# First mixer of a two-layer trunk: a group's outputs are issued in pieces between the next group's weight blocks, and VectorE's steps of the solve get precedence

## The chip, the cores and the metric

The kernel runs on one core of one Trainium2 chip. The metric is the device time of one execution in microseconds (us). Engines in the text: TensorE (PE in the rows, with PEld for its weight loads), VectorE (DVE), ScalarE (ACT), GpSimd (POOL) and SyncE (SP), which here only issues transfers.

## The reference

The program is a decoder trunk of two layers on 256 tokens of width 2048, in float32. The change is in the mixer of the first layer, a gated delta rule:

```python
qkv, z, a, b = jnp.split(x @ w_in, ...)
qkv = jax.nn.silu(causal_dwconv(qkv, conv_w))
q, k = l2norm(q) * GDN_DK ** -0.5, l2norm(k)
...
lmat = jnp.where(strict, einsum(kb, k) * decay, 0.0)
sol  = triangular_solve(lmat + eye, rhs, lower=True, unit_diagonal=True)
...
v_new = u_n - einsum(w_n, S)
o_n   = einsum(qd_n, S) + einsum(qk_n, v_new)
...
o = o * rsqrt(mean(square(o)) + RMS_EPS) * norm_g * silu(z)
return o @ w_o
```

There are 32 value heads and 16 key heads of 128; then follow layer norm, a gated feed-forward part, a second mixer (sparse attention) and a second feed-forward part, none of which the diff touches.

## The kernel before

All products with weights are done in two parts. A weight block of 512 KB arrives as `raw` (SyncE issues it, line 103), ScalarE rounds it to `hi` (line 107), VectorE makes `lo = raw - hi` (line 108), and TensorE multiplies both. `raw`, `hi` and `lo` have three buffers each, and the two conversions are issued with a large precedence, so they run about three blocks ahead of TensorE. Products with the weights on the left write `mm_ps` (lines 126 and 130), those with the weights on the right write `b_ps` (lines 150, 151 and 154).

The mixer works through eight groups of four value heads. `keys(g)` makes q and k, `front(g)` makes the decays, the triangular blocks and their inverses of 32 x 32 (GpSimd's long chain at lines 505 and 507), `values(g)` makes v from eight weight blocks and transposes it (`v_ps`, `vt`), `zgate(g)` makes the gate z from eight more, `inverses(g)` fetches the small inverses (`pm<-tt`) and multiplies them (`w_ps`), `solve(g)` solves for `u` in two halves a = 0 and 1 (`s_ps`, `y`, `u`), and `outputs(g)` makes for each half the product `o_ps`, its squares (`sqs`, ScalarE), a reciprocal root in small VectorE steps (`rs`, `rt`, lines 243 to 249), the scaled tile `ot`, its transposes `ot_ps`, and the two parts of `oT`, which the projection with `w_o` reads after the mixer.

A scheduler orders the instructions of each engine: among those it thinks ready, the one written first goes first, or the one with precedence. Each engine then works through its list strictly in that order. What the scheduler thinks ready can be late on the chip.

Two details matter below. The tile `qd` has two buffers: the read of the decays of group g + 2 (`qd<-grow`, line 414, on SyncE's list) must wait until `o_ps` of group g has been made, because that reads the old `qd`; and ScalarE's `qo<-qd,go` (line 419) waits for that read. The blocks of `L` go through DRAM to another layout: four stores `lt<-L` (line 489), one load `ld<-lt` (line 492), both on SyncE's list among the weight blocks; then GpSimd starts its chain.

Of the kernel before, what the change touches and what calls it, by code (L numbers as in the profile page):

```python
# [12 lines left out]
ALU = mybir.AluOpType  # L13
# [43 lines left out]
def bcast(ap, n, axis):  # L57

    dims = [list(x) for x in ap.ap]
    dims.insert(axis, [0, n])  # L60
    return bass.AP(tensor=ap.tensor, offset=ap.offset, ap=dims)


class Trunk:
# [313 lines left out]
    def gdn_groups(self, pool, gk, cw, ng, oT, load, gates):  # L378
# [1 line left out]

        nc, t = self.nc, self.t
        w_in = t["gdn_w_in"]
        pm = pool.tile([P, 8, P], F32, tag="pm", name="pm")
        nc.gpsimd.memset(pm, 0.0)
# [5 lines left out]
        h4 = range(4)  # L392
        five = lambda ap: ap.rearrange("p (j r) t -> p j r t", r=2)

        def conv(n0, out):

            def done(n, ps):
                pd = pads[n % 2]
                self.fold(pool, pd[:, 3:], ps)
                ac = pool.tile([P, S], F32, tag="ac", name="ac", bufs=2)  # L400
                w = cw[:, :, n0 + n]
                nc.scalar.activation(ac, pd[:, 3:], AF.Identity, scale=w[:, 3:4])
                for k in (2, 1, 0):
                    nc.vector.scalar_tensor_tensor(ac, pd[:, k:k + S], w[:, k:k + 1], ac, op0=ALU.mult, op1=ALU.add)
                o = out(n)
                nc.scalar.activation(o, ac, AF.Tanh, scale=0.5)
                nc.vector.scalar_tensor_tensor(o, o, 1.0, ac, op0=ALU.add, op1=ALU.mult)
            return done

        def decays(s):  # L410

            g = s["g"]
            dm = s["qd"] = pool.tile([P, 2, 4, P], F32, tag="qd", name="qd", bufs=2)
            nc.sync.dma_start(out=dm, in_=bass.AP(tensor=self.grow.tensor, offset=self.grow.offset + 4 * g * P,
                                                    ap=[[0, P], [32 * P, 2], [1, 4 * P]]))
            do = s["qo"] = pool.tile([P, 4, P], F32, tag="qo", name="qo", bufs=2)
            L = s["L"] = pool.tile([P, 2, 4, P], F32, tag="L", name="L")
            for h in h4:
                nc.scalar.activation(do[:, h], dm[:, 1, h], AF.Exp, bias=self.gout[:, 4 * g + h:4 * g + h + 1])
            for a in range(2):  # L420
                for h in h4:
                    gc = self.gc[:, a, 4 * g + h:4 * g + h + 1]
                    nc.vector.tensor_scalar(L[:, a, h], dm[:, a, h], gc, 0.0, op0=ALU.subtract, op1=ALU.max)
                    nc.vector.tensor_scalar(dm[:, a, h], dm[:, a, h], gc, 0.0, op0=ALU.subtract, op1=ALU.min)
                nc.scalar.activation(L[:, a], L[:, a], AF.Exp, scale=-1.0)
                nc.scalar.activation(dm[:, a], dm[:, a], AF.Exp)
                nc.gpsimd.tensor_tensor(dm[:, a], dm[:, a], bcast(self.tri, 4, 1), op=ALU.mult)

        def keys(g):
            s = {"g": g}  # L430
            q = s["q"] = pool.tile([P, 2, S], F32, tag="q", name="q")
            k = s["k"] = pool.tile([P, 2, S], F32, tag="k", name="k")
            steps = (self.gemm_t_steps(w_in, 2048 + 256 * g, 256, self.xT, conv(16 + 2 * g, lambda n: k[:, n])),
                     self.gemm_t_steps(w_in, 256 * g, 256, self.xT, conv(2 * g, lambda n: q[:, n])))
            if not g:
                for nb in range(4):
                    load(nb)
                    next(steps[0])
                gates()
            for x in steps:  # L440
                self.go_(x)
            return s
# [71 lines left out]
        def mul(lhs, rhs, ps=None, first=True, last=True):  # L514
            ps = ps if ps is not None else self.sp.tile([P, 4, P], F32, tag="bk", name="s_ps")
            for h in h4:
                nc.tensor.matmul(ps[:, h], lhs[:, h], rhs[:, h], start=first, stop=last)  # L517
            return ps
# [8 lines left out]
                mul(s["L"][:, a], pm[:, 4 * a:4 * a + 4, 32:], ps)  # L527
                nc.scalar.activation(W[:, a, :, 32:], ps, AF.Copy)

        def values(s):  # L530
            g, sv = s["g"], s["sv"]
            v = pool.tile([P, 4, S], F32, tag="v", name="v")
            self.gemm_t(w_in, 4096 + 512 * g, 512, self.xT, conv(32 + 4 * g, lambda n: v[:, n]))
            vt = s["vt"] = pool.tile([P, 2, 4, P], F32, tag="vt", name="vt")
            for a in range(2):
                ps = self.sp.tile([P, 4, P], F32, tag="sp", name="v_ps")
                for h in h4:
                    nc.tensor.transpose(ps[:, h], v[:, h, a * P:(a + 1) * P], self.ident)
                for h in h4:
                    nc.scalar.activation(vt[:, a, h], ps[:, h], AF.Identity, scale=sv[:, a, h // 2, h % 2:h % 2 + 1])  # L540
# [10 lines left out]
        def solve(s):  # L551
            vt = s["vt"]
            u = s["u"] = pool.tile([P, 2, 4, P], F32, tag="u", name="u")
            for a in range(2):
                rhs = vt[:, a]
                if a:
                    ps = mul(s["n21"], u[:, 0])
                    for h in h4:
                        nc.vector.scalar_tensor_tensor(rhs[:, h], ps[:, h], s["nc1"][:, h:h + 1], rhs[:, h],
                                                       op0=ALU.mult, op1=ALU.add)  # L560
                y0 = pool.tile([P, 4, P], F32, tag="y0", name="y0")
                nc.scalar.activation(y0, mul(pm[:, 4 * a:4 * a + 4], rhs), AF.Copy)
                y = y0
                for i in range(3):
                    ps = mul(W[:, a], y)
                    y = u[:, a] if i == 2 else pool.tile([P, 4, P], F32, tag="y", name="y", bufs=2)
                    nc.vector.tensor_tensor(y, y0, ps, op=ALU.subtract)

        def outputs(s):

            g, u = s["g"], s["u"]
            ss = pool.tile([P, 2, 2, 2], F32, tag="oss", name="oss", bufs=2)
            f = pool.tile([P, 2, 2, 2], F32, tag="of", name="of", bufs=2)
            for a in range(2):
                ps = self.sp.tile([P, 4, P], F32, tag="bk", name="o_ps")
                for h in h4:
                    if a:
                        nc.tensor.matmul(ps[:, h], s["qo"][:, h], u[:, 0, h], start=True, stop=False)
                    nc.tensor.matmul(ps[:, h], s["qd"][:, a, h], u[:, a, h], start=not a, stop=True)
                sq = pool.tile([P, P], F32, tag="sqs", name="sqs")  # L580
                for h in h4:
                    nc.scalar.activation(sq, ps[:, h], AF.Square, accum_out=ss[:, a, h // 2, h % 2:h % 2 + 1])
                nc.vector.scalar_tensor_tensor(f[:, a], ss[:, a], 1.0 / 128, bcast(s["wq"][:, :, a], 2, 2),
                                               op0=ALU.mult, op1=ALU.add)
                fa = self.rsqrt(pool, f[:, a].rearrange("p j r -> p (j r)"), 4)
                ot = pool.tile([P, 4, P], F32, tag="y", name="ot", bufs=2)
                for h in h4:
                    nc.vector.scalar_tensor_tensor(ot[:, h], ps[:, h], fa[:, h:h + 1], s["zs"][:, a, h * P:(h + 1) * P],
                                                   op0=ALU.mult, op1=ALU.mult)
                ps = self.sp.tile([P, 4, P], F32, tag="bk", name="ot_ps")  # L590
                for h in h4:
                    nc.tensor.transpose(ps[:, h], ot[:, h], self.ident)
                hi = oT[:, 4 * g:4 * g + 4, 0, a * P:(a + 1) * P]
                lo = oT[:, 4 * g:4 * g + 4, 1, a * P:(a + 1) * P]
                nc.scalar.activation(hi, ps, AF.Identity, scale=ng)
                nc.vector.scalar_tensor_tensor(lo, ps, ng, hi.bitcast(F32), op0=ALU.mult, op1=ALU.subtract)

        def front(s):
            decays(s)
            sums(s)  # L600
            blocks(s)

        n = keys(0)
        front(n)
        for g in range(8):
            s = n
            values(s)
            zgate(s)
            if g < 7:
                n = keys(g + 1)  # L610
            inverses(s)
            if g < 7:
                front(n)
            solve(s)
            outputs(s)


    def project(self, pool, src, h, kt, g, b, prepare, side=1):
# [300 lines left out]
```

## Time and profile before

| what | value |
|---|---|
| median of 3 runs (lowest to highest) | 2909.66 us (2909.45 to 2909.71) |
| the profiled execution, time | 2910.35 us |
| its span, first to last instruction | 2908.3 us |
| TensorE matmul busy | 2823.9 us, 97% |
| VectorE busy | 1873.8 us, 64% |
| ScalarE busy | 1394.7 us, 48% |
| GpSimd busy | 399.7 us, 14% |
| mean granted TensorE clock | 0.992 of full |

Busy times are those of the one profiled execution. The mixer takes the first 800 us of the span. Nearly all of the kernel is bound by TensorE, so a change shows in the time only where TensorE itself waits, or where it is made to wait. The `w_ps` of successive groups stand some 89 us apart.

### The profile page before, as it was taken

How to read it: one execution, taken by the hardware profiler on the slowest of the kernel's cores; microseconds unless marked ns; L12 is line 12 of the kernel's file. 1: busy time of each engine (PE TensorE's matmuls, PEld its weight loads, DVE VectorE, ACT ScalarE, POOL GpSimd, SP SyncE). 2: the span in 40 equal slices, each digit the busy share in tenths (PEclk: the TensorE clock that was granted, in tenths of full speed). 3: DMA queues.
4: the chain of work that ended last, by engine and by line, in shares of the span. 5: the costliest groups of instructions: out<-in, count | busy, mean ns of one | idle time of the engine just before them, and what ended most of it. 6: DMA issues, size and time to landing. Idle time of an engine off the chain costs nothing.

```text
span 2908.3 us, 41890 instructions
## 1 busy us (share of the span) xinstructions
PE 2823.9 (97%) x15790; PEld 2444.7 (84%) x15790; DVE 1873.8 (64%) x3148; ACT 1394.7 (48%) x2147; POOL 399.7 (14%) x720
## 2 busy tenths in 40 slices
PE   8799999999799999999999999999999999999998
PEld 6688888888689888888888878888888888888887
DVE  6578777788455666666545665666576666654465
ACT  4445455554333655555433543455365555543353
POOL 1543354543300000000000000120000000000000
PEclk9899999999899999999999999999999999999999
DMA  7555556555375566666655556554556666655555
GB/s 196 152 135 153 160 157 172 156 149 156 95 227 189 168 194 202 206 205 202 197 193 193 184 185 196 168 166 139 190 168 192 192 195 196 195 190 195 189 189 180
DMA packets 425947, 520.94 MB, mean 179 GB/s; under 512 B 28268, under 2 KB 329712, under 8 KB 425488
## 3 DMA queue, kind: packets, MB, share of 16 engines
q1 hardware_dynamic: 418576, 499.91, 56.3%
q0 software_dynamic: 7168, 18.35, 2.8%
q8 instruction: 124, 2.03, 0.3%
q14 instruction: 79, 0.65, 0.1%
HBM read 513.94 MB, written 7.39 MB: 179 GB/s over the span
## 4 chain that ended last, share of the span: by engine, by line
PE 69%; issue 2%; DMA 2%; DVE 2%; ACT 1%; POOL 1%; DVEq 0%; SPq 0%; POOLq 0%; ACTq 0%
PE mm_ps L126 25%; PE mm_ps L130 13%; PE b_ps L154 10%; PE b_ps L150 9%; PE b_ps L151 9%; DMA lnb<-in_ln_b 1%; DVE lo L108 1%; ACT hi L107 1%; POOL xt L505 1%; PE s_ps L517 0%; POOL xi L507 0%; PE sc_ps L792 0%; DMA ld<-lt 0%; PE lg_ps L842 0%; DMA lng<-in_ln_g 0%
## 5 line engine op out<-in xcount | busy, mean ns | idle before, releaser
L108 DVE TENSOR_TENSOR lo<-raw,hi 128x1024 fp32r<-128x1024 f32 x925 | 1137.4, 1231 | 826.9 <-ACT hi L107 806.2
L107 ACT ACTIVATE hi<-raw 128x1024 fp32r<-128x1024 f32 x925 | 977.5, 1057 | 1279.3 <-PE b_ps L151 539.4
L126 PE MATMUL mm_ps<-xT,hi 128*128 128x512 f32 x4176 | 1062.0, 395 | 3.0 <-DVE rs L243 1.7
L126 PEld LDWEIGHTS mm_ps<-xT,hi 128*128 128x128 f32 x4176 | 750.6, 189 | 138.0 <-issue 2.7
L130 PEld LDWEIGHTS mm_ps<-xT,lo 128*128 128x128 f32 x4176 | 572.7, 190 | 39.5
L130 PE MATMUL mm_ps<-xT,lo 128*128 128x256 f32 x4176 | 600.8, 284 | 0.0
L150 PE MATMUL b_ps<-hi,xT 128*128 128x512 f32 (+2 forms) x736 | 274.6, 379 | 2.4 <-ACT sg L718 2.4
L151 PE MATMUL b_ps<-hi,xT 128*128 128x512 f32 (+2 forms) x736 | 275.3, 379 | 0.0
L150 PE MATMUL b_ps<-hi,hTA 128*128 128x512 f32 (+1 forms) x640 | 212.4, 347 | 0.0
L151 PE MATMUL b_ps<-hi,hTA 128*128 128x512 f32 (+1 forms) x640 | 212.3, 347 | 0.0
L154 PE MATMUL b_ps<-lo,xT 128*128 128x512 f32 (+2 forms) x736 | 194.6, 382 | 1.7 <-DVE lo L108 1.7
L203 POOL DMA_DIRECT2D lng<-in_ln_g x16 | 8.7, 546 | 1116.9 <-DVE lo L108 562.8
L150 PEld LDWEIGHTS b_ps<-hi,xT 128*128 128x128 f32 x736 | 138.9, 189 | 27.5 <-ACT sg L718 3.7
L151 PEld LDWEIGHTS b_ps<-hi,xT 128*128 128x128 f32 x736 | 139.5, 190 | 23.7
L154 PEld LDWEIGHTS b_ps<-lo,xT 128*128 128x128 f32 x736 | 131.8, 189 | 26.1 <-DVE lo L108 2.5
L154 PE MATMUL b_ps<-lo,hTA 128*128 128x512 f32 (+1 forms) x640 | 138.6, 347 | 0.0
L150 PEld LDWEIGHTS b_ps<-hi,hTA 128*128 128x128 f32 x640 | 121.2, 189 | 15.0
L151 PEld LDWEIGHTS b_ps<-hi,hTA 128*128 128x128 f32 x640 | 121.2, 189 | 14.9
L505 POOL TENSOR_TENSOR xt<-ld,xi 128x60 f32<-128x60 f32 (+24 forms) x248 | 118.3, 477 | 93.5 <-DMA ld<-lt 74.7
L507 POOL TENSOR_TENSOR xi<-xi,xt 128x60 f32<-128x60 f32 (+24 forms) x248 | 115.3, 465 | 19.4
L154 PEld LDWEIGHTS b_ps<-lo,hTA 128*128 128x128 f32 x640 | 105.1, 189 | 15.0
L150 PE MATMUL b_ps<-hi,oT 128*128 128x512 f32 (+1 forms) x320 | 106.9, 349 | 0.0
(260 smaller groups left out, 2660.1 us busy)
## 6 DMA issues: line engine op xcount, KB each, us to landing
raw<-in_gdn_w_in SPq DMA_DIRECT2D x193, 512.0 KB, 3.9
raw<-in_ffn_w_gate SPq DMA_DIRECT2D x160, 512.0 KB, 4.5
raw<-in_ffn_w_up SPq DMA_DIRECT2D x160, 512.0 KB, 4.5
raw<-in_ffn_w_down SPq DMA_DIRECT2D x160, 512.0 KB, 3.6
raw<-in_dsa_w_in SPq DMA_DIRECT2D x80, 512.0 KB, 3.6
raw<-in_gdn_w_o SPq DMA_DIRECT2D x64, 512.0 KB, 4.0
raw<-in_ple_w_gate SPq DMA_DIRECT2D x64, 512.0 KB, 4.1
raw<-in_dsa_w_o SPq DMA_DIRECT2D x32, 512.0 KB, 3.6
```

The lines of the kernel that those rows point to most:

```text
L107: nc.scalar.activation(hi, raw, AF.Copy)
L108: ins = nc.vector.tensor_tensor(lo, raw, hi.bitcast(F32), op=ALU.subtract)
L126: nc.tensor.matmul(q[:m, :], hi[:, k, o:o + m], x[:, k0 + k].rearrange("p a b -> p (a b)"), start=k0 + k == 0, stop=False)
L130: nc.tensor.matmul(q[:m, S:], lo[:, k, o:o + m], x[:, k0 + k, 0, :], start=False, stop=k0 + k == kt - 1)
L150: nc.tensor.matmul(ps[a][:, :n], xh, hi[:, k, :], start=k0 + k == 0, stop=False)
L151: nc.tensor.matmul(ps[a][:, :n], xl, hi[:, k, :], start=False, stop=False)
L154: self.last = nc.tensor.matmul(ps[a][:, :n], x(k0 + k)[:, 0, a * P:(a + 1) * P], lo[:, k, :], start=False, stop=k0 + k == kt - 1)
L203: ins = self.nc.gpsimd.dma_start(out=r, in_=bass.AP(tensor=src.tensor, offset=src.offset, ap=[[0, P], [1, n]]))
L505: nc.gpsimd.tensor_tensor(tmp[:, :m, :w], bcast(ld[:, i + 1:, i], m, 1), xi[:, :m, i:i + 1].to_broadcast([P, m, w]), op=ALU.mult)
L507: nc.gpsimd.tensor_tensor(xi[:, :m, i + 1:], xi[:, :m, i + 1:], tmp[:, :m, :w], op=ALU.subtract)
```

## The change

`outputs(s)` becomes a generator that stops after the tile `ot` of each half. It is no longer run behind `solve(s)`; the next group's `values` runs it in three pieces: the first ahead of its weight blocks, the second (transposes of half 0, and half 1 up to `ot`) behind the third block, the third (transposes of half 1) behind the sixth. For the last group the pieces run one after the other at the end. In `solve`, three kinds of VectorE instructions (the right side `vt` of half 1, each `y`, and `u`) are issued with precedence over what was written before them.

```diff
-        def values(s):
+        def values(s, side):
             g, sv = s["g"], s["sv"]
             v = pool.tile([P, 4, S], F32, tag="v", name="v")
-            self.gemm_t(w_in, 4096 + 512 * g, 512, self.xT, conv(32 + 4 * g, lambda n: v[:, n]))
+            next(side, None)
+            for i, _ in enumerate(self.gemm_t_steps(w_in, 4096 + 512 * g, 512, self.xT,
+                                                    conv(32 + 4 * g, lambda n: v[:, n]))):
+                if i % 3 == 2:
+                    next(side, None)
...
                 if a:
                     ps = mul(s["n21"], u[:, 0])
-                    for h in h4:
-                        nc.vector.scalar_tensor_tensor(rhs[:, h], ps[:, h], s["nc1"][:, h:h + 1], rhs[:, h],
-                                                       op0=ALU.mult, op1=ALU.add)
+                    with tc.high_priority():
+                        for h in h4:
+                            nc.vector.scalar_tensor_tensor(rhs[:, h], ps[:, h], s["nc1"][:, h:h + 1], rhs[:, h],
+                                                           op0=ALU.mult, op1=ALU.add)
...
                     ps = mul(W[:, a], y)
                     y = u[:, a] if i == 2 else pool.tile([P, 4, P], F32, tag="y", name="y", bufs=2)
-                    nc.vector.tensor_tensor(y, y0, ps, op=ALU.subtract)
+                    with tc.high_priority():
+                        nc.vector.tensor_tensor(y, y0, ps, op=ALU.subtract)
...
                     nc.vector.scalar_tensor_tensor(ot[:, h], ps[:, h], fa[:, h:h + 1], s["zs"][:, a, h * P:(h + 1) * P],
                                                    op0=ALU.mult, op1=ALU.mult)
+                yield
...
+        side = iter(())
         for g in range(8):
             s = n
-            values(s)
+            values(s, side)
...
             solve(s)
-            outputs(s)
+            side = outputs(s)
+        for _ in side:
+            pass
```

The lists of all engines are the same up to the first group's `s_ps` for half 1, and again from each group's second half of `zgate` to the next group's solve; what changes lies between, in seven places of the same pattern (groups 0 to 6), of which the last differs only in that no further decays are read. Behind the last `zgate` the lists are the same to the end of the program. New line numbers are up to 10 higher.

**First place.** ScalarE, second half of a group's outputs (shown for group 5; `vt` and `v` are of group 6, `qo<-qd,go` of group 7). Before:

```order
L595 ACTIVATE oT<-ot_ps,ng 128x4x128
L406 ACTIVATE v<-ac 128x256 x2
L582 ACTIVATE sqs,oss<-o_ps 128x128 x4
L540 ACTIVATE vt<-v_ps,sv 128x128 x6
L107 ACTIVATE hi<-raw 128x1024
L540 ACTIVATE vt<-v_ps,sv 128x128 x2
L419 ACTIVATE qo<-qd,go 128x128 x4
L107 ACTIVATE hi<-raw 128x1024
```

Now, at the same place:

```order
L588 ACTIVATE sqs,oss<-o_ps 128x128 x2
L107 ACTIVATE hi<-raw 128x1024
L588 ACTIVATE sqs,oss<-o_ps 128x128
L406 ACTIVATE v<-ac 128x256
L588 ACTIVATE sqs,oss<-o_ps 128x128
L406 ACTIVATE v<-ac 128x256
L419 ACTIVATE qo<-qd,go 128x128
L107 ACTIVATE hi<-raw 128x1024
L544 ACTIVATE vt<-v_ps,sv 128x128 x8
L419 ACTIVATE qo<-qd,go 128x128
L107 ACTIVATE hi<-raw 128x1024
```

The first `qo` has moved ahead of a `hi` and of all eight `vt`.

**Second place.** VectorE, the end of the reciprocal root of half 1 and the tile `ot` (the same group; the numbers in `rs` and `rt` name buffers). Before:

```order
L247 TENSOR_TENSOR rt_6317<-rs_6316 128x4
L248 TENSOR_TENSOR rt_6317<-rt_6317,of 128x4
L249 SCALAR_TENSOR_TENSOR rs_6316<-rt_6317,rs_6316 128x4
L108 TENSOR_TENSOR lo<-raw,hi 128x1024
L588 SCALAR_TENSOR_TENSOR ot<-o_ps,rs_6316,zs 128x128 x4
```

Now:

```order
L248 TENSOR_TENSOR rt_6386<-rt_6386,of 128x4
L108 TENSOR_TENSOR lo<-raw,hi 128x1024
L249 SCALAR_TENSOR_TENSOR rs_6385<-rt_6386,rs_6385 128x4
L247 TENSOR_TENSOR rt_6386<-rs_6385 128x4
L248 TENSOR_TENSOR rt_6386<-rt_6386,of 128x4
L249 SCALAR_TENSOR_TENSOR rs_6385<-rt_6386,rs_6385 128x4
L594 SCALAR_TENSOR_TENSOR ot<-o_ps,rs_6385,zs 128x128 x4
```

Four small steps of the root now stand behind the `lo`. That `lo` is, in both lists, the one of the `hi` that the first place shows last before (between the `vt`) and right behind the first `qo` now. On TensorE's list, 23 matmuls `b_ps` and four transposes `v_ps` stood between the last `o_ps` of half 1 and the first `ot_ps` of half 1; now it is 30 and four.

**Third place.** VectorE in the solve of group 5 and the front of group 6 (`u`, `y` and `vt` belong to the solve; `L`, `n` and `qd` to the front). Before:

```order
L484 SCALAR_TENSOR_TENSOR L<-g_ps,c,L 128x128 x7
L108 TENSOR_TENSOR lo<-raw,hi 128x1024
L484 SCALAR_TENSOR_TENSOR L<-g_ps,c,L 128x128
L494 TENSOR_TENSOR n_6115<-g_ps,qo 128x512
L567 TENSOR_TENSOR u<-y_6199,s_ps 128x512
```

Now:

```order
L484 SCALAR_TENSOR_TENSOR L<-g_ps,c,L 128x128 x2
L573 TENSOR_TENSOR u<-y_6199,s_ps 128x512
L484 SCALAR_TENSOR_TENSOR L<-g_ps,c,L 128x128 x4
L564 SCALAR_TENSOR_TENSOR vt<-s_ps,nc_5123,vt 128x128 x4
L108 TENSOR_TENSOR lo<-raw,hi 128x1024
L484 SCALAR_TENSOR_TENSOR L<-g_ps,c,L 128x128 x2
L494 TENSOR_TENSOR n_6115<-g_ps,qo 128x512
```

The solve's `u` and `vt` now stand ahead of the last six and the last two of the eight `L`. On SyncE's list the order around it was, before:

```order
L103 DMA raw<-in_gdn_w_in 128x2x512 x2
L489 DMA lt<-L 32x8x32 x4
L103 DMA raw<-in_gdn_w_in 128x2x512
L492 DMA ld<-lt 128x1x1024
L103 DMA raw<-in_gdn_w_in 128x2x512 x4
L414 DMA qd<-grow 128x2x512
```

Now:

```order
L103 DMA raw<-in_gdn_w_in 128x2x512 x2
L489 DMA lt<-L 32x8x32 x4
L492 DMA ld<-lt 128x1x1024
L103 DMA raw<-in_gdn_w_in 128x2x512 x4
L414 DMA qd<-grow 128x2x512
```

The weight block between the stores `lt` and the load `ld` now stands behind `ld`, so that one block fewer is issued ahead of `qd<-grow`.

## Rows read from the trace of the kernel before

**Rows 1.** TensorE's waits in the first 800 us: total, times, longest.

```profile
PE w_ps L517 <- DMA pm<-tt: 31.3, 2, 16.4
...
PE ot_ps L592 <- DVE ot L588: 7.0, 16, 0.7
PE s_ps L517 <- DVE y L567: 6.3, 7, 1.0
```

**Rows 2.** TensorE, 632 to 650: start, duration, line, operation, [idle before].

```profile
638.09 0.71 PE L154 MATMUL b_ps<-lo,xT 128*128 128x512 f32 x2
...
641.86 0.39 PE L150 MATMUL b_ps<-hi,xT 128*128 128x512 f32 x1
...
643.67 0.39 PE L154 MATMUL b_ps<-lo,xT 128*128 128x512 f32 x1
644.48 0.30 PE L592 MATMUL ot_ps<-ident,ot 128*128 128x128 f32 x1 [0.42 <-DVE ot L588]
```

**Rows 3.** ScalarE, 635 to 662.

```profile
638.43 0.28 ACT L582 ACTIVATE sqs<-o_ps 128x128 f32<-128x128 f32 x1 [0.30 <-PE o_ps L579]
...
638.83 0.28 ACT L582 ACTIVATE sqs<-o_ps 128x128 f32<-128x128 f32 x1
...
644.06 1.28 ACT L419 ACTIVATE qo<-qd,go 128x128 f32<-128x128 f32 x4 [1.04 <-DMA qd<-grow]
645.24 1.04 ACT L107 ACTIVATE hi<-raw 128x1024 fp32r<-128x1024 f32 x1
```

**Rows 4.** SyncE's issues of transfers, 610 to 662.

```profile
638.37 0.37 SPq L414 DMA_DIRECT2D qd<-grow  x1
```

**Rows 5.** Transfers: count, KB each, us to landing; 180 to 770, then 275 and 362.

```profile
raw<-in_gdn_w_in SPq DMA_DIRECT2D x148, 512.0 KB, 3.8
qd<-grow SPq DMA_DIRECT2D x6, 512.0 KB, 5.7
...
qd<-grow SPq DMA_DIRECT2D x1, 512.0 KB, 5.5
...
qd<-grow SPq DMA_DIRECT2D x1, 512.0 KB, 6.1
```

**Rows 6.** VectorE, 628 to 650.

```profile
642.44 0.16 DVE L248 TENSOR_TENSOR rt<-rt,of 128x4 f32<-128x4 f32 x1
642.64 0.16 DVE L249 SCALAR_TENSOR_TENSOR rs<-rt,rs 128x4 f32<-128x4 f32 x1
642.75 1.33 DVE L108 TENSOR_TENSOR lo<-raw,hi 128x1024 fp32r<-128x1024 f32 x1
644.00 1.11 DVE L588 SCALAR_TENSOR_TENSOR ot<-o_ps,rs,zs 128x128 f32<-128x128 f32 x4
```

**Rows 7.** VectorE, 690 to 760.

```profile
702.03 0.35 DVE L484 SCALAR_TENSOR_TENSOR L<-g_ps,c,L 128x128 f32<-128x128 f32 x1
...
702.89 0.68 DVE L567 TENSOR_TENSOR u<-y,s_ps 128x512 f32<-128x512 f32 x1
...
706.97 1.12 DVE L559 SCALAR_TENSOR_TENSOR vt<-s_ps,nc,vt 128x128 f32<-128x128 f32 x4
...
724.70 1.78 DVE L404 SCALAR_TENSOR_TENSOR ac<-pd,cw,ac 128x256 f32<-128x256 f32 x4
```

**Rows 8.** TensorE, 690 to 800.

```profile
715.77 2.09 PE L126 MATMUL mm_ps<-xT,hi 128*128 128x512 f32 x8
717.70 1.12 PE L130 MATMUL mm_ps<-xT,lo 128*128 128x256 f32 x8
```

**Rows 9.** SyncE's issues, 680 to 765.

```profile
702.56 1.94 SPq L489 DMA_DIRECT2D lt<-L  x4
...
707.65 0.53 SPq L492 DMA_DIRECT2D ld<-lt  x1
```

**Rows 10.** TensorE, 1738 to 1756.

```profile
1746.94 1.92 PE L197 MATMUL t_ps<-ident,x 128*128 128x128 f32 x8 [1.62 <-DVE x L720]
```

**Rows 11.** Busy time in a stretch: PE, PEld, DVE, ACT, POOL, granted clock, DMA share, GB/s.

```profile
1746.00:1750.00 4.00, 3.06 (x15) 3.09 (x16) 2.56 (x5) 1.32 (x3) 1.97 (x4) 0.62 0.55 141
```

More of the change, by code (lines that the diff above doesn't have):

```diff
@@ L378, in gdn_groups @@
     def gdn_groups(self, pool, gk, cw, ng, oT, load, gates):
-        nc, t = self.nc, self.t
+        nc, tc, t = self.nc, self.tc, self.t
         w_in = t["gdn_w_in"]
```

## The prediction

> **What bounds the kernel now.** I read the waits of TensorE first, since an engine that is busy for nearly all of the span gives back only its own idle time. In the first 800 us, where the mixer lies, the list is short [rows 1]: two long waits for the small inverses (`w_ps`, 31.3 us together), sixteen short ones for the scaled outputs (`ot_ps`, 7.0 us, so 0.44 each, two in every group), and seven of about 0.9 us for the first `y` of a solve. The change can earn at most what stands there. The two long waits belong to groups 0 and 7. The first lies ahead of everything the change moves. The second, 16.4 us, ends when GpSimd's chain of group 7 is through; it swallows whatever TensorE wins or loses between group 7's front and its `w_ps`. So of the seven places of the pattern the last counts only through the start of that chain, and six count in full. The 0.9 us wait of the solve stands at a point where the lists of all engines are as before, so I leave it. What is left to win is the `ot_ps` waits of groups 0 to 5: twelve of 0.44, or 5.3 us, 0.18%.
>
> Next I read one group's outputs on TensorE, ScalarE, SyncE and VectorE, in a window of 20 us, to see what each `ot` waits for.
>
> **Half 1 of the outputs, the term that decides.** All times here count from the moment at which TensorE is past the last `o_ps` of half 1, 638.09 [rows 2]. Before, `ot_ps` starts at 644.48, that is at +6.39, of which 0.42 is waiting: TensorE is there at +5.97 [rows 2]. ScalarE starts its squares at +0.34 and takes 0.40 for one with its readout [rows 3]; then come `vt`, a `hi`, and the four `qo`, which begin at 644.06 (+5.97) after an idle 1.04 spent on the read of the decays [rows 3]. That read could not be issued before `o_ps` was done: SyncE issues it at 638.37, +0.28 [rows 4]. It needs 5.7 us to land in the median of six, 5.5 and 6.1 in two of them, where a weight block of the same 512 KB needs 3.8 [rows 5]. Before, this wait hurts nobody: the `hi` whose `lo` stands ahead of `ot` is already made.
>
> In the changed order the first `qo` stands ahead of that `hi` (the first place shown above). ScalarE reaches it after four squares, one `hi` of about 1 us and two `v` of about 0.35 (an estimate, from the 0.30 of a `qo` with half their columns): 0.34 + 1.6 + 1.0 + 0.7 = +3.6. It then stands until the read has landed. With 5.7 us that is +5.97 as before. One `qo` takes 0.30 (1.18 us for four) and the `hi` 1.04 [rows 3], so it is ready at +7.3. VectorE's `lo` follows and holds the engine for about 1.2 us (642.75 to 644.00) [rows 6]: +8.5. Behind it stand four small steps of the root at 0.20 each (642.44 to 642.64) [rows 6]: `ot` starts at +9.3. TensorE's first transpose starts 0.48 us after `ot` (644.00 and 644.48) [rows 6, 2]: +9.8, which is 3.4 later than before. TensorE for its part arrives later too: seven more `b_ps` matmuls stand ahead of the transposes, at 0.226 each (1.81 us for eight) [rows 2], 1.6 us, so it arrives at +7.55. The wait grows from 0.42 to 2.2 us: **1.8 us lost in each group**.
>
> This price hangs on when the read lands. In the new order the next weight block is issued later behind it, so that it may be a little quicker; I take 5.5, the shortest of the six, and a loss of 1.6. Bounds: if the read landed as fast as a weight block, in 3.8, ScalarE would stand for only half a microsecond, and the loss would be 0 (3.4 - 1.9 - 1.6); at 6.1 it is 2.2.
>
> The Trainium skill, in DMA: Bandwidth & Descriptors, "Anatomy of one DMA", puts a transfer (through GpSimd's path) at about 2 us plus its bytes over 436 GB/s. By this the read would land after 3.2 us (an estimate from that page), ScalarE would hardly wait, and the time would be that of the rival called faster below; the rows have 5.5 and more, so the trace does not agree, and the sum goes by the rows.
>
> **Half 0 of the outputs.** On VectorE there stand, from `o_ps` of half 0 to `ot`, the solve's `u` (0.6), six `ac` at 0.44 (1.78 us for four) [rows 7], two `lo` of 1.2, two `v` of 0.4 (an estimate, from the `ac` of the same size) and thirteen small steps of 0.1 to 0.2 [rows 6], some 8.6 us, and 0.48 to the first transpose. TensorE now has `o_ps` itself (some 0.8), then 4 + 8 + 8 `hi` matmuls at 0.241 (715.77 to 717.70 for eight) and 8 + 8 + 7 half-width ones at about 0.12 (1.12 for eight with the tail) [rows 8]: about 8.4 us. So TensorE waits about 0.7 where it waited 0.44: **0.2 us lost in each group**. Bounds: 0.44 won, if `ot` comes in time, and 0.8 lost, if the squares, now broken by a `hi` of 1 us, end that much later.
>
> **The solve.** Precedence for `u`, `vt` and `y` wins nothing on TensorE, because behind the first `y` no step of the solve appears among its waits [rows 1]. Each `y` and `u` is ready 0 to 0.3 us ahead of its matmuls also in the new order, as far as I can follow it by the same durations. If every one of the six came a little late, it would cost up to 0.3 per group; I take 0.
>
> **The start of the last chain.** The precedence puts `u` (0.68 us) and `vt` (1.12) ahead of the last `L`, which ended at 702.38 [rows 7]: about 1.4 us later, with the slot in which VectorE stood idle for a `hi`. The stores `lt`, issued at 702.56 [rows 9], move with it. Against that, the load `ld`, issued at 707.65 [rows 9], no longer has to stand behind a weight block that would take 3.8 us to land [rows 5]. Between 1.4 lost and 2.4 won I take 0; it counts once, for group 7, whose long wait covers 16.4 us. The other groups have the 89 us of a whole group for their chain.
>
> **The sum.** 6 x (1.6 + 0.2) = 10.8 us. The profiled execution took 2910.35, 0.69 above the median of the three runs, 2909.66; on the median this makes 2920.5, 0.37% slower. The measurement can tell about 0.2%, 5.8 us, from no change.
>
> **Rivals.**
>
> *The read lands in time, or its wait is covered.* Speaking for it: the blocks on either side of the read are issued at other times, and weight blocks of its size take 3.8. Against it: all six took 5.5 or more. The halves' losses would be 0 to 0.7 in each group, the total 2908 to 2915. The same time would come out if the generator's pieces only moved work that other work covers: no difference to be measured.
>
> *Faster.* The place is the same `ot`, by one mechanism: if ScalarE got through to the `hi` by +3.9, `ot` would start near +7.4 or before, TensorE would find it done, and all twelve waits of groups 0 to 5 would go. That wins 5.3 us, with the quicker `ld` 7.7: 2902 to 2904. It decides where the read takes under 3.4 us, and no row has that.
>
> *The clock falls in the new gaps.* TensorE stood for 1.62 us ahead of 1746.94 [rows 10], and in 1746 to 1750 the granted clock averaged 0.62, that is, most of it at the lower level of 1.2 GHz [rows 11]; 0.38 x 4 = 1.5 us of work were lost. A gap of 2 us in six groups could bring six such falls, 9 us on top: 2929. Against it, the short waits in the mixer had no such effect, and here full-width matmuls stand on both sides of the gap. TensorE: Matmul & The Clock Gate of the Trainium skill, "HAM oscillation", describes the drop for repeated waits of TensorE between bursts; the row of 1746 shows one here, behind a wait shorter than those that page tells of.
>
> **How the numbers follow.** The read's wait, at 6 to 17 us lost: 0.65, and its likeliest time is 2920.5. With falls of the clock, 2926 and above: 0.10. Covered or small: 0.20. Faster: 0.05. Slower by over 0.2% (above 2915.5) takes the first two: 0.75; within 0.2%: 0.20. The range leaves out one in ten at each side: from 2911, in the covered case, to 2927, with some falls of the clock.
>
> **What would show it.** In the changed profile ScalarE's wait for `qd<-grow` ahead of `qo` should rise from about 1 us to 2 or more in groups 0 to 5; TensorE's waits of `ot_ps` for `ot` should rise from 7.0 us to some 17 to 20, with the longest about 2; the second long wait for `pm` should end at about the same distance from the last `L`. The prediction is wrong if the read lands within 4.5 us in the new order, if the `lo` ahead of `ot` turns out not to belong to the `hi` behind `qo`, or if a wait that I hold to be covered, in the solve, opens in every group.

## The result, and the profile after

The changed kernel takes 2934.2 us in the median (2928.7 to 2943.8), the kernel before 2909.7 in the same measurement: a ratio of 1.0088, with a 95% interval of 1.0076 to 1.0100. It is slower, as forecast, but by 24.5 us where 10.8 were forecast, and outside the range of 2911 to 2927. The profiled execution took 2928.74 us with a span of 2926.7.

TensorE's waits in the first 800 us (total, times, longest), which answer to [rows 1]:

```profile
PE w_ps L517 <- DMA pm<-tt: 26.1, 2, 13.2
PE ot_ps L599 <- DVE ot L594: 23.8, 21, 2.5
...
PE s_ps L517 <- DVE y L573: 6.3, 7, 0.9
...
PE v_ps L542 <- DVE v L407: 3.3, 7, 0.6
```

The wait for `ot` rose from 7.0 us to 23.8, and from 16 times to 21: there are new ones. A wait for `v` is new too. The second long wait became shorter (12.9 in place of 16.4), because TensorE arrives later at it; the first (13.2 in place of 14.9) lies ahead of the change and differs from one execution to the next.

What a group costs is read from five whole groups, from `w_ps` of group 1 to `w_ps` of group 6. First the row of before, then that of after (length; busy time of PE, PEld, DVE, ACT, POOL; granted clock, DMA share, GB/s):

```profile
233.90:678.90 445.00, 434.09 (x2563) 376.63 (x2562) 353.76 (x795) 232.37 (x451) 202.75 (x374) 1.00 0.58 159
```

```profile
234.90:700.80 465.90, 439.70 (x2563) 379.27 (x2562) 357.07 (x795) 234.21 (x451) 200.10 (x374) 0.99 0.56 152
```

The five groups take 20.9 us more, 4.2 each, and group 0 some 2.7 (from its `w_ps`, at 140.1 before and 138.4 now). In the five, TensorE is idle for 26.2 us in place of 10.9, and busy 5.6 us longer with the same 2563 matmuls. This execution, the fastest of the six, ends 18.4 us later than the profiled one of before (spans 2926.7 and 2908.3).

One place per group, as before group 5's. TensorE, 647 to 666 (start, duration, [idle before]):

```profile
648.65 0.31 PE L599 MATMUL ot_ps<-ident,ot 128*128 128x128 f32 x1 [0.72 <-DVE ot L594]
...
652.87 0.33 PE L599 MATMUL ot_ps<-ident,ot 128*128 128x128 f32 x1 [1.98 <-DVE ot L594]
...
654.74 0.48 PE L151 MATMUL b_ps<-hi,xT 128*128 128x512 f32 x1
...
659.32 0.95 PE L542 MATMUL v_ps<-ident,v 128*128 128x128 f32 x4 [0.45 <-DVE v L407]
664.10 0.30 PE L599 MATMUL ot_ps<-ident,ot 128*128 128x128 f32 x1 [0.85 <-DVE ot L594]
```

The first and last `ot_ps` here belong to half 0 and half 1. The second is the last transpose of half 0, and its wait of 1.98 is the new one: in groups 0 to 5 it is 1.53, 0.86, 1.46, 1.17, 2.46 and 1.98, 9.5 us. Half 1, the term that was to decide, waits 0.84, 0.85, 0.64, 0.86, 2.34 and 0.85, not 2.2 each.

What the new wait waits for stands on VectorE, ScalarE and SyncE, here in this order:

```profile
648.15 0.87 DVE L594 SCALAR_TENSOR_TENSOR ot<-o_ps,rs,zs 128x128 f32<-128x128 f32 x3
651.32 1.23 DVE L108 TENSOR_TENSOR lo<-raw,hi 128x1024 fp32r<-128x1024 f32 x1 [2.30 <-ACT hi L107]
652.47 0.34 DVE L594 SCALAR_TENSOR_TENSOR ot<-o_ps,rs,zs 128x128 f32<-128x128 f32 x1
```

```profile
650.23 1.06 ACT L107 ACTIVATE hi<-raw 128x1024 fp32r<-128x1024 f32 x1 [4.82 <-DMA raw<-in_gdn_w_in]
```

```profile
633.32 1.84 SPq L489 DMA_DIRECT2D lt<-L  x4
637.40 0.53 SPq L492 DMA_DIRECT2D ld<-lt  x1
639.89 13.06 SPq L103 DMA_DIRECT2D raw<-in_gdn_w_in  x4
```

Three of the four `ot` steps are done, then VectorE stands 2.30 us for a `hi`, which stood 4.82 us for the weight block that SyncE issued right behind `ld`, at 639.89. The block was there at 650.2, 10.3 us later. In the kernel before the same block stood ahead of `ld` and landed in 4.1 us. There too the block that stands next behind `ld` lands late, after 8.3 to 9.5 us in five groups for which the trace tells it; the longest landing of before, from 180 to 760 us:

```profile
DMA to landing us min/median/max: 3.4/3.8/9.5
```

But that block is one further on, and ScalarE comes to its `hi` only 10.9 us after its issue (622.15 and 633.07 in group 5). Now the late block is the one before it, and ScalarE stands ready 5.5 us after its issue. In the kernel before no `hi` of the mixer's middle (170 to 770 us) waits for a transfer; now, on ScalarE:

```profile
ACT hi L107 <- DMA raw<-in_gdn_w_in: 27.8, 6, 5.4
...
ACT qo L419 <- DMA qd<-grow: 12.9, 6, 3.0
```

The last chain. VectorE's last `L`, SyncE's `lt` and `ld`, GpSimd's first step and TensorE's `w_ps` of group 7:

```profile
725.34 0.60 DVE L484 SCALAR_TENSOR_TENSOR L<-g_ps,c,L 128x128 f32<-128x128 f32 x2
...
725.97 1.84 SPq L489 DMA_DIRECT2D lt<-L  x4
730.30 0.53 SPq L492 DMA_DIRECT2D ld<-lt  x1
...
741.45 0.25 POOL L505 TENSOR_TENSOR xt<-ld,xi 128x31 f32<-128x31 f32 x1 [7.53 <-DMA ld<-lt]
...
783.40 0.93 PE L517 MATMUL w_ps<-pm,L 128*128 128x96 f32 x3 [12.90 <-DMA pm<-tt]
```

and in the kernel before GpSimd's first step and the same `w_ps`:

```profile
719.44 1.22 POOL L505 TENSOR_TENSOR xt<-ld,xi 128x31 f32<-128x31 f32 x1 [9.94 <-DMA ld<-lt]
...
761.92 3.48 PE L517 MATMUL w_ps<-pm,L 128*128 128x96 f32 x15 [16.42 <-DMA pm<-tt]
```

From the last `L` to `w_ps` it is 57.5 us now and was 59.5 [rows 7].

### The profile page after: what moved, and what is told of

The parts are those of the page before. It is cut to its first block, busy times and chain, and to the rows that moved or that the text cites. A ratio compares the mean times of both kernels' runs of the same rounds, so it can differ in the third digit from the quotient of the medians.

```text
span 2926.7 us, 41870 instructions
## 1 busy us (share of the span) xinstructions
PE 2830.5 (97%) x15790; PEld 2446.8 (84%) x15790; DVE 1879.3 (64%) x3148; ACT 1397.0 (48%) x2147; POOL 395.9 (14%) x720
## 4 chain that ended last, share of the span: by engine, by line
PE 81%; DVE 6%; DMA 5%; issue 3%; ACT 2%; POOL 2%; SPq 0%; DVEq 0%; ACTq 0%; POOLq 0%
PE mm_ps L126 29%; PE mm_ps L130 15%; PE b_ps L154 10%; PE b_ps L150 10%; PE b_ps L151 10%; DVE lo L108 2%; PE s_ps L517 2%; DMA raw<-in_gdn_w_in 2%; ACT hi L107 1%; POOL xt L505 1%; POOL xi L507 1%; DMA lnb<-in_ln_b 1%; DMA ld<-lt 1%; DMA qd<-grow 1%; PE w_ps L517 1%
## 5 line engine op out<-in xcount | busy, mean ns | idle before, releaser
L505 POOL TENSOR_TENSOR xt<-ld,xi 128x60 f32<-128x60 f32 (+24 forms) x248 | 110.9, 447 | 79.4 <-DMA ld<-lt 60.6
```

The lines of the kernel that those rows point to most:

```text
L505: nc.gpsimd.tensor_tensor(tmp[:, :m, :w], bcast(ld[:, i + 1:, i], m, 1), xi[:, :m, i:i + 1].to_broadcast([P, m, w]), op=ALU.mult)
```

## The experiments

Times are medians; beside each stands the ratio to the kernel before, measured in the same session (2909.0 in the first four, 2910.2 in the next four, 2910.1 in the last three). Some facts of the programs come first. The pieces without the precedence give the lists of the kernel before on all five engines, and the precedence without the pieces gives those of the changed kernel, so the whole change of the order comes from the precedence. Precedence for `y` alone gives the lists of before. With `u` alone, `vt` alone, or both without `y`, the weight block stays ahead of `ld`: that swap needs all three together. The pieces:

```diff
-                    with tc.high_priority():
...
-                    with tc.high_priority():
```

> The change's first part alone: the outputs run in three pieces between the weight blocks, no precedence in the solve. The lists of all five engines come out in the order of the kernel before. Theory (the loss comes from what the precedence reorders): 2909.7, within 2 us of the kernel before. Rival (the pieces themselves cost time): some of the 24.5 us lost, 2914 or more.

2909.3 us, ratio 0.9999 (0.9990 to 1.0008). The pieces cost and give nothing.

**ld on GpSimd's queue.**

```diff
-            nc.sync.dma_start(out=ld, in_=...)
+            nc.gpsimd.dma_start(out=ld, in_=...)
```

> The changed kernel with the load ld issued by GpSimd, which waits for it anyway, in place of SyncE; nothing else moves on TensorE, VectorE and ScalarE. Theory (the weight block behind ld on SyncE's list lands 10.8 us after its issue, so that hi, lo and the last ot of half 0 come late): ScalarE's waits for raw from 170 to 770 fall from 27.8 us in 6 to under 5, the second ot_ps wait of half 0 (9.5 us in groups 0 to 5) goes to under 1.5, and the time falls by 9 to 14 with the clock falls behind these gaps: 2920 to 2925. Rival 1 (TensorE waits because the interleaved lists of VectorE and ScalarE are longer, whatever the queue does): the waits stay, 2932 to 2936. Rival 2 (the 16 DMA engines are the limit and not the order of the queue): the block lands after 8 us or more all the same, 2929 to 2934.

2939.1 us, ratio 1.0097 (1.0082 to 1.0112): worse, and no theory foresaw it. One group's rows, VectorE, GpSimd and ScalarE:

```profile
645.32 3.76 DVE L108 TENSOR_TENSOR lo<-raw,hi 128x1024 fp32r<-128x1024 f32 x1
```

```profile
645.48 2.51 POOL L512 TENSOR_TENSOR L<-L,cst 128x512 f32<-128x512 f32 x2
```

```profile
656.73 1.06 ACT L107 ACTIVATE hi<-raw 128x1024 fp32r<-128x1024 f32 x1 [3.28 <-DMA raw<-in_gdn_w_in]
```

GpSimd issues `ld` at 644.74, and the `lo` that VectorE begins at 645.32 takes 3.76 us where it took 1.45 in the changed kernel. In each of the seven groups this `lo` ends 1.1 us after GpSimd's two steps on `L`, which now stand behind the issue of `ld` on GpSimd's list; whether the issue or these steps hold it up no run separates. The `lo` frees the buffer of the next block, so that the block is issued 8.9 us behind `lt` in place of 6.6. So the edit brought a cost of its own. It shows two things all the same: taking `ld` from SyncE's list does not help by itself, and a block issued 4.4 us behind `ld` still lands late, after 6.9 to 8.3 us, though `ld` is on another queue. The order within SyncE's queue alone is not what makes a block late; in this, rival 2 came near.

**qo behind ot.**

```diff
+                ins = nc.scalar.activation(do[:, h], dm[:, 1, h], AF.Exp, bias=...)
+                self.ot and self.after(ins, self.ot)
```

> The changed kernel with ScalarE's four qo put behind the ot of half 1 by an ordering edge; only ScalarE's list differs. Theory (qo's wait for the read of the decays, ahead of hi, delays half 1): the first ot_ps wait of half 1 falls from 0.64 to 0.86 (2.34 once) to about 0.45 in every group, a gain of 2 to 4 us and one clock fall, 2928 to 2932; ScalarE's wait for qd shrinks from 12.9 us to under 3. Rival (half 1 is late for VectorE's longer list and not for qo): the waits stay as they are, 2933 to 2936. If the step of the prediction that priced this at 1.6 in each group were right after all, the gain would be near 10, 2924.

2928.2 us, ratio 1.0060 (1.0047 to 1.0073): 19.2 us over the kernel before, where the changed kernel lies 24.5 over it, so 5.3 better. `ot_ps` of half 1 in group 5 now waits as it did before the change:

```profile
663.05 0.30 PE L599 MATMUL ot_ps<-ident,ot 128*128 128x128 f32 x1 [0.43 <-DVE ot L594]
```

ScalarE's waits for `qd` are gone from the list of 170 to 770 us. So the predicted mechanism is there, at about 5 us with all that follows from it, not 9.6. ScalarE's waits for `raw` stayed (32.0 us in this run).

**Both edits**, the two diffs above together.

> Both edits together. Theory: what is left of the loss is the first ot_ps wait of half 0 (0.4 more in each group) and the wait for v (0.45): 2.5 to 5 us, so 2912 to 2917, if no clock falls remain. Rival (the interleaving itself costs, or a quicker block only moves the wait to the next one): 2922 or more.

2934.1 us, ratio 1.0085 (1.0072 to 1.0099): a miss, for the reason found above. Against `ld` on GpSimd's queue alone it is 5.0 us better, which agrees with the 5.3 that `qo` gave alone.

**The block ahead of ld again.** The load is written behind the solve, and waits for its last `u` (`self.u`):

```diff
+            s["fetch"] = lambda: nc.sync.dma_start(out=ld, in_=...)
...
+            ins = s["fetch"]()
+            s["g"] in (0, 7) or self.after(ins, self.u, True)
```

> The changed kernel with ld, in groups 1 to 6, made to wait for the solve's last u, so that SyncE issues the weight block first and ld right behind it; all other lists are those of the changed kernel. Theory A (ld's 512 KB ahead of the block on the DMA engines make it land 10 us after its issue): the block, still issued some 6.6 us behind lt, lands in about 5, ScalarE's waits for raw go from 27.8 us to under 5, the second ot_ps wait of half 0 (9.5 us in groups 0 to 5) goes, with the clock falls behind it: 2920 to 2925. Theory B (the block is late because VectorE's lo, which frees its buffer, now stands behind the solve's steps): the block's issue stays 2 us late, the waits stay above 15 us, 2930 or more.

2921.6 us, ratio 1.0039 (1.0027 to 1.0051): 11.4 us over the kernel before, 13.1 better than the changed kernel. SyncE in the same place of group 5, and the landing times of the blocks from 600 to 660 us, as far as the trace tells them:

```profile
625.17 1.87 SPq L489 DMA_DIRECT2D lt<-L  x4
631.78 0.39 SPq L103 DMA_DIRECT2D raw<-in_gdn_w_in  x1
632.41 0.54 SPq L492 DMA_DIRECT2D ld<-lt  x1
```

```profile
DMA to landing us min/median/max: 3.6/3.7/5.3
```

The same line of the changed kernel:

```profile
DMA to landing us min/median/max: 3.7/3.9/10.3
```

The block at 631.78 landed in 3.6 us (the 5.3 is that of a later one); behind `ld` it needed 10.3. It is still issued 6.6 us behind `lt`, and yet ScalarE's waits for `raw` fell from 27.8 to 6.6 us, so theory B falls. The second `ot_ps` wait of half 0 is gone in groups 0 to 5, and no fall of the clock stands between the two long waits; `ot_ps` waits fell from 23.8 to 14.8.

**The same with qo behind ot**, this diff and that of `qo` together.

> The edit of the run before together with the qo behind ot, which alone gave 6 us. Theory A: 2914 to 2920, what is left being the first ot_ps wait of half 0 (0.4 us more in each group) and the wait for v (0.45 each); theory B: 2925 or more.

2925.5 us, ratio 1.0056 (1.0042 to 1.0071): a miss; it should have been better than the run before. `ot_ps` waits fell to 9.3 us, but TensorE now waits for the inverses in the middle groups as well (170 to 760 us):

```profile
PE w_ps L521 <- DMA pm<-tt: 5.5, 5, 1.4
```

`ld` starts 7.2 us behind `lt` in the run with the block ahead, 4.1 in the changed kernel, and GpSimd's chain of a middle group has no 3 us to spare once TensorE is quicker. That takes back 4.7 us (the run before had 0.8 of such waits) of the 5.5 won at `ot_ps`; why the median is 3.9 us above the run before, and not just level with it, it does not show.

**ld first, in the kernel before.** Weight blocks take an ordering edge; in groups 1 to 6 the third block of the next `zgate` stands behind `ld`:

```diff
+        dma = nc.sync.dma_start(out=raw, in_=src[...])
+        to = self.hold.pop() if self.hold else None; to and self.after(dma, to)
...
+            self.hold = [s["ld"], None, None] if 0 < s["g"] < 7 else []
```

> The kernel before, with one thing of the change alone: in groups 1 to 6 the weight block stands behind ld on SyncE's list, by an ordering edge; all other lists are those of before. Theory A: the block lands about 10 us after its issue in place of about 5, ScalarE waits for raw some 3 to 5 us in each of six groups, VectorE's lo and the u behind it come late, TensorE waits 2 to 5 us in each group: 2920 to 2940. Theory B: no difference, 2908 to 2912.

2926.1 us, ratio 1.0055 (1.0043 to 1.0067). One swap of two transfers on SyncE's list costs 16 us in six groups. SyncE, the landing times (600 to 660), ScalarE and TensorE of group 5:

```profile
626.23 2.00 SPq L489 DMA_DIRECT2D lt<-L  x4
630.30 0.53 SPq L492 DMA_DIRECT2D ld<-lt  x1
630.93 15.86 SPq L103 DMA_DIRECT2D raw<-in_gdn_w_in  x4
```

```profile
DMA to landing us min/median/max: 3.6/3.8/13.1
```

```profile
644.08 1.06 ACT L107 ACTIVATE hi<-raw 128x1024 fp32r<-128x1024 f32 x1 [2.62 <-DMA raw<-in_gdn_w_in]
```

```profile
648.89 0.50 PE L592 MATMUL ot_ps<-ident,ot 128*128 128x128 f32 x2 [2.52 <-DVE ot L588]
```

**Precedence for u alone, and for vt alone.**

```diff
-                    with tc.high_priority():
+                    with tc.high_priority() if i == 2 else nullcontext():
                         nc.vector.tensor_tensor(y, y0, ps, op=ALU.subtract)
```

> The changed kernel with precedence for u alone (vt and y without). The lists then have the block ahead of ld as in the kernel before, u ahead of the last six L, and the four qo ahead of a hi. Theory A: no wait of ScalarE for raw behind ld, so at most the smaller losses: 2909 to 2918. Rival (precedence for u is what costs, by what it moves on VectorE): 2922 or more.

> The changed kernel with precedence for vt alone (u and y without). The lists have the block ahead of ld as in the kernel before, but the first qo ahead of a hi as in the changed kernel. If precedence costs mostly by the place of ld, this stands near the run with u alone, 2915 to 2922; if qo ahead of hi carried the loss, as the prediction had it, 2918 to 2925 with ot_ps waits of half 1 near 2 us; if neither costs much, 2909 to 2914.

With `u` 2919.9 us, ratio 1.0029 (1.0018 to 1.0041); with `vt` 2914.7, ratio 1.0011 (1.0001 to 1.0020). In both the block stands ahead of `ld`, and neither has a wait of ScalarE for it. TensorE's `ot_ps` waits in the first 800 us with `vt`, and the five groups with `u`:

```profile
PE ot_ps L599 <- DVE ot L594: 6.4, 15, 0.6
```

```profile
237.10:689.80 452.70, 439.31 (x2563) 375.33 (x2562) 357.67 (x795) 234.08 (x451) 198.84 (x374) 1.00 0.56 156
```

With `vt` alone the first `qo` stands ahead of a `hi` as in the changed kernel, and yet half 1 waits only 0.2 to 0.3 us in groups 0 to 5: the place of `qo` alone does not make the loss. ScalarE has one `hi` more ahead of it there and waits 0.4 to 1.1 us for `qd`. With `u` alone no `ot_ps` wait is over 0.5 us, and yet five groups take 7.7 us more than before. Of these 2.5 are idle time; 5.2 are in busy time, with the same matmuls at the full clock. That is what many waits too short to be listed would look like, but no run shows whose they are.

**Holding the blocks where TensorE waits anyway.** In the kernel before, with `hold` as above but a real wait for GpSimd's first step of the chain (`first`), in groups 0 and 7, and in group 7 alone:

```diff
+            self.hold = [s["first"]] + [None] * {0: 6, 7: 2}[s["g"]] if s["g"] in (0, 7) else []
```

> The kernel before, and for groups 0 and 7 alone, whose w_ps is waited for (14.9 and 16.4 us), the next weight block made to wait until ld has landed, so that ld stands first and has the DMA engines to itself. TensorE's own wait for the later blocks is swallowed by the two long waits. Theory (the 10 to 12 us from ld's issue to the chain's first step are the sharing with weight blocks): ld lands in 5 to 6 us, each long wait ends 4 to 6 us earlier, 2898 to 2903, faster than both kernels. Rival (ld's 512 KB from DRAM are slow by themselves): 1 us or less in each group, 2907 to 2910. Third: the held blocks stall TensorE for longer than the long waits cover, 2912 or more.

> The same in group 7 alone; SyncE's list there is the only list that changes. Theory: half the gain, 2903 to 2906. Rival: 2908 to 2910.

Both groups: 2907.7 us, ratio 0.9993 (0.9984 to 1.0001), short of the theory's 2898 to 2903. Group 7 alone: 2906.8, ratio 0.9988 (0.9979 to 0.9998), 3.3 us below the kernel before, with the interval's end all but at no change. SyncE, GpSimd and TensorE of the latter:

```profile
705.12 1.94 SPq L489 DMA_DIRECT2D lt<-L  x4
709.36 0.53 SPq L492 DMA_DIRECT2D ld<-lt  x1
719.23 1.41 SPq L103 DMA_DIRECT2D raw<-in_gdn_w_in  x3
```

```profile
718.95 0.25 POOL L505 TENSOR_TENSOR xt<-ld,xi 128x31 f32<-128x31 f32 x1 [6.95 <-DMA ld<-lt]
```

```profile
761.25 2.00 PE L517 MATMUL w_ps<-pm,L 128*128 128x96 f32 x8 [10.52 <-DMA pm<-tt]
```

With no weight block issued beside it, `ld` still needs 9.6 us from issue to the chain's first step, against 11.8 before (707.65 [rows 9] to 719.44). The rival was nearer: the transfer is slow by itself, and sharing explains 2 us of it. From `lt` to `w_ps` it is 56.1 us in place of 59.4 (761.25 - 705.12, 761.92 - 702.56 [rows 9]), which agrees with the 3.3 us of the medians.

## Why the prediction was right in sign and wrong in size

**The step that failed** is "the start of the last chain": it saw that the weight block now stands behind `ld`, priced what `ld` gains by it in group 7, and did not follow the block. The block lands in 9.1 to 10.7 us in place of 3.6 to 4.1, in each of six groups, and VectorE's list has its `lo` between the third and the fourth `ot` of half 0. Undoing this one swap gives 13.1 us back, making it in the kernel before costs 16. The step on half 0 inherited the error: it summed VectorE's work up to the first `ot`, and so came to 0.2 lost in each group. That wait did rise to 0.72 to 0.92 (forecast 0.7), but the last transpose, behind the late `lo`, then waits 1.6 on average, which the sum did not have.

**Half 1** was right in mechanism and mis-sized. ScalarE's waits for `qd` rose from 6.5 us in six (170 to 770) to 12.9, "from about 1 us to 2 or more", as forecast. But the read landed in 4.9 us in the median of six, not 5.5, and TensorE came to `ot_ps` at +8.5 (664.10 - 0.85 - 654.74), not +7.55; 0.45 of that is its wait for `v` on the way. `ot` let it start at +9.4, forecast +9.8. The wait is 0.85, and putting `qo` behind `ot` gains some 5 us instead of 9.6.

**The solve** at 0 holds: `s_ps` waits 6.3 us as before. **The start of the last chain**, as a term of the sum, came out at a gain of 2.1 from `L` to `w_ps`, with the last `L` later, 25.1 us behind `w_ps` of group 6 in place of 23.5 (725.94 - 700.80, 702.38 - 678.90); 0 was right for the two together, -0.4.

**The sign that was to confirm it** misled: that the waits of `ot_ps` "should rise from 7.0 us to some 17 to 20, with the longest about 2" was nearly met (23.8 and 2.5), but more by a wait at another transpose (9.5 us) than by the two that were forecast. The place tells the cause, not the total.

**The rival of the falling clock** came true in part. Behind the gaps of 2.46 and 2.34 in group 4, of 556 to 560 and 570 to 574 (the sixth value is the granted clock):

```profile
556.00:560.00 4.00, 3.79 (x18) 3.78 (x19) 3.46 (x9) 1.49 (x4) 3.22 (x10) 0.57 0.45 131
...
570.00:574.00 4.00, 4.00 (x13) 3.13 (x13) 2.48 (x4) 1.78 (x4) 3.43 (x8) 0.57 0.55 149
```

0.43 x 4, twice, is 3.4 us lost in this execution, of the 5.6 by which TensorE's busy time grew. The executions nearest the median had a mean granted clock of 0.990, where this one had 0.992: 0.002 of 2934 us, some 6 us (an estimate, known to 3 us by the rounding), where the median lies 5.5 us above this execution. So the falls cost the median execution likely some 9 us in all, which is what the rival named and the sum left out.

**What stays open.** The block behind `ld` (13.1) and `qo` (5.3) make 18.4 of the 24.5 us, each known to some 5 us, as the intervals of two ratios allow. They were not had together: with both undone TensorE waits for GpSimd's chain in the middle groups, whose 89 us the prediction took for ample. And `u` alone costs 9.8 us by waits that the views do not resolve.

## What to carry to other kernels

When a change reorders a queue, follow every transfer that moved, not only the one that gains: a block that moves behind a slow load inherits its landing time, and where its turn comes sooner than that, the engine that converts it hands the delay to whatever stands behind it in its list. Precedence given to a chain takes it from someone; find whose buffer comes free later. A wait forecast by place and size is confirmed only at its place.

## What the runs showed of the hardware

`ld` moves 512 KB, as a weight block does, and needs 9.2 to 9.6 us to the chain's first step with no block beside it; a block needs 3.8. Issued by GpSimd it landed in 10.2 us in the median of seven. The Trainium skill, in DMA: Bandwidth & Descriptors, "Anatomy of one DMA", has about 3.2 us for this size on that path (an estimate from its formula); the runs do not agree. With `ld` alone in flight the DMA share is 0.25, the work of four of the 16 engines, and with weight blocks alone it is 0.98 (the last two values are DMA share and GB/s; from the run that holds group 7's block):

```profile
713.00:717.00 4.00, 4.00 (x31) 3.70 (x30) 3.92 (x9) 1.37 (x2) 0.00 (x0) 1.00 0.25 78
...
721.00:723.00 2.00, 2.00 (x14) 1.77 (x13) 1.00 (x6) 0.03 (x1) 1.61 (x6) 1.00 0.98 370
```

The pattern of `ld` reads the same data four times, with the four copies outermost; whether the four engines follow from that no run tests.

A block behind `ld` lands at about the time at which `ld` is through, and not a fixed time after its own issue. In groups 1 to 7, as far as the traces tell it, it landed in 11.9 to 13.1 us when issued 0.6 us behind `ld` (the kernel before with `ld` first), in 9.1 to 10.7 at 2.2 to 2.6 (changed kernel), and in 8.3 to 9.5 at 3.0 to 3.5 (kernel before). Each time that is 11.6 to 13.7 us behind the issue of `ld`, whose data the chain's first step uses after 10.5 to 13.1. That a block waits for its share on the engines that `ld` occupies would fit this; no run shows it engine by engine.

A gap of 2 to 3 us on TensorE was followed by a fall of the clock in some places and not in others. In the kernel before with `ld` first, TensorE stood 2.01, 3.15, 2.42, 2.24 and 2.52 us ahead of `ot_ps`; the 4 us behind the first, the second and the last (the sixth value is the granted clock):

```profile
191.20:195.20 4.00, 4.00 (x15) 3.15 (x16) 3.54 (x8) 1.48 (x2) 3.45 (x8) 0.58 0.49 154
374.40:378.40 4.00, 3.98 (x28) 3.55 (x29) 4.00 (x9) 2.29 (x4) 3.45 (x8) 1.00 0.49 155
...
648.90:652.90 4.00, 4.00 (x14) 3.07 (x15) 3.58 (x8) 1.12 (x2) 3.45 (x8) 0.57 0.49 157
```

The first and the last two were mostly at the lower level (0.57 to 0.58), the second, behind the longest gap, and the third at the full one. With `ld` on GpSimd's queue two of seven such gaps (2.67 to 2.89) had a fall behind them. The executions of the changed kernel spread over 15 us, those of the kernel before over 3.5 in the same session (over 9.7 in 26 executions of a later one). The mean granted clock goes with it: 0.992 in the fastest of the changed kernel, 2928.74 us, and 0.988 in the slowest, 2943.76. 0.004 of 2940 us is some 12 of the 15 us (an estimate), so most of the spread is the clock.
